# The second FFN product of a two-layer diffusion backbone as seven quarter products in place of eight

## The chip, the cores and the metric

The kernel runs on one core of a Trainium2 chip. The metric is device time in microseconds (us) of one execution. The kernel before takes 1958.51 us, the median of three runs (1956.71 to 1959.27).

An engine's name in the profile: PE is TensorE's matmuls, PEld its weight loads, DVE is VectorE, ACT is ScalarE, POOL is GpSimd, SP is the queue that issues the loads from device memory. L240 is line 240 of the kernel whose profile is shown.

## The reference

Two post-norm layers over 512 latent tokens (the second layer) or 512 latent and 256 context tokens (the first), with D = 1024. Each layer has a token mixer, gated linear attention in layer 0 and Mamba-2 in layer 1, and then an MLP with a squared ReLU, D_FF = 4096:

```python
def sq_relu_mlp(h, w1, w2):
    return jnp.square(jax.nn.relu(h @ w1)) @ w2
...
hl = layer_norm(DEEPNORM_ALPHA * hl + m_l[5] * sq_relu_mlp(modulate(hl, m_l[3], m_l[4]), ffn_w1[i], ffn_w2[i]),
                ln_g[i, 1], ln_b[i, 1])
```

`m_l` and `m_c` are rows of six modulation vectors ("ada"), a product of the conditioning vector with a matrix of 1024 x 6144 per layer. The change touches `@ w2` alone, in both layers.

## The kernel before

All data lie transposed: features on the 128 partitions, tokens along the columns. A tile of features is 128 of them, so D has 8 tiles and D_FF 32. A matmul takes a 128 x 128 block of weights and up to 512 token columns. In layer 0 the 768 tokens take two matmuls, of 512 and of 256 columns; in layer 1 the 512 tokens take one.

**Split products.** Every operand x is kept as two fp32r tensors, `xh` (x rounded by a cast on ScalarE) and `xl` (what is left, a subtraction on VectorE): `split_to`. A product is three matmuls, wh xh + wh xl + wl xh, all in line 240 (`prod`). Weights arrive in one of four buffers `raw` (512 KB, 128 x 1024 floats), and ScalarE's cast (L203) and VectorE's subtraction (L204) make `wh` and `wl`, three buffers each. The same four `raw` buffers serve W1, W2 and the ada matrix, taken in turn; a load is issued when the last reader of its buffer has ended.

**The FFN** (`ffn`, L363). An "f1 tile" is one of the 32 tiles of the first product, 8 x 3 matmuls per piece of tokens. Behind it come: relu out of PSUM on ScalarE (`rr`, L384), the square on GpSimd (`rq`, L385), the square's rounded part on ScalarE (`rh`, L386) and the rest on VectorE (`rl`, L387). The tiles of D_FF are then the k tiles of the second product. They are worked in five blocks of 8, 8, 8, 8 - n and n (n is 3 in layer 0, 2 in layer 1): all f1 tiles of a block, then for each of 8 output tiles the product with W2 over the block's k tiles and an addition of it, times the gate, to the residual `acc` in SBUF (`accum_proj`, VectorE, L419). The last n tiles go through `accum_last`, in pieces of 256 tokens, so that the layer norm of one piece overlaps the product of the next.

**What sets the order.** Each engine runs its instructions in the order of the program, and loads stand in one queue (SP). A scheduler that places the program's instructions by priority makes this order. Ada rows are spread over the other work: `worked` counts matmul columns, and after every `pace` units of 768 columns it advances `background` by a step, which loads 512 KB of the ada matrix and multiplies and sums them on VectorE (L157), once for the latent conditioning and, in the rows that the context needs too, a second time. The generators in `side` (layer norms) are advanced in the same way.

## Time and profile before

| | |
|---|---|
| median of the runs | 1958.51 us (1956.71 to 1959.27) |
| the profiled execution | span 1959.6 us |
| TensorE busy | 1881.3 us, 96% of the span |
| VectorE, ScalarE, GpSimd busy | 64%, 41%, 21% |
| bytes moved | 219.01 MB, 112 GB/s mean |
| FFN of layer 0, FFN of layer 1 | about 440 to 980 us; about 1600 to 1937 us |

The profiled execution is 1.1 us longer than the median. In the rows that follow, a group of instructions is given as: line, engine, operation, output<-inputs, their shapes, count | busy us, mean ns of one | idle time of the engine just ahead of them, and what ended it. In a timeline a row begins with the start in us from the span's start and the duration. The granted TensorE clock (PEclk) is 1.00 at full speed.

### The profile page before, as it was taken

The page shows a single profiled execution, that of the slowest core. Times are in us where ns is not written, and L with a number is a line of the kernel's source. Part 1 is how long each engine was busy: PE and PEld are TensorE (multiplying, and loading weights), DVE is VectorE, ACT ScalarE, POOL GpSimd, SP SyncE. Part 2 cuts the span into 40 slices and gives each one's busy share as a digit, 9 for nine tenths or more (in the row PEclk, how much of TensorE's full clock was granted, in tenths as well). Part 3 has the DMA queues.
Part 4 walks back from the last instruction along what each step waited for, and adds up shares of the span by engine and source line. Part 5 has one row for each costly group of instructions (what it writes and reads, how often), then busy time and mean ns, then how long its engine had stood idle before and what let it go on. Part 6 is the DMA issues. An engine that isn't in the chain of part 4 may idle for free.

```text
span 1959.6 us, 29026 instructions
## 1 busy us (share of the span) xinstructions
PE 1881.3 (96%) x11405; PEld 1604.9 (82%) x11405; DVE 1254.9 (64%) x1929; ACT 798.6 (41%) x1386; POOL 410.8 (21%) x448
## 2 busy tenths in 40 slices
...
GB/s 329 156 73 114 104 36 106 65 55 150 141 142 140 138 137 135 116 41 116 33 107 121 129 115 112 104 101 129 121 100 132 164 73 105 96 99 96 96 89 54
DMA packets 78936, 219.01 MB, mean 112 GB/s; under 512 B 11056, under 2 KB 15792, under 8 KB 78800
## 3 DMA queue, kind: packets, MB, share of 16 engines
...
## 4 chain that ended last, share of the span: by engine, by line
PE 63%; DVE 13%; DMA 7%; ACT 6%; POOL 5%; issue 5%; SPq 0%; DVEq 0%; POOLq 0%; ACTq 0%
PE mm L240 54%; DMA L<-crowc 4%; POOL L L1001 1%; ACT L L998 1%; DMA raw<-in_ada_wr_dram 1%; DVE A L593 1%; PE sm L943 1%; DVE raw L157 1%; DVE cv L867 1%; POOL L L912 1%; PE sm L676 1%; DVE wl L204 1%; POOL W L612 1%; PE sm L986 1%; PE mm L520 1%
## 5 line engine op out<-in xcount | busy, mean ns | idle before, releaser
L240 PE MATMUL mm<-xh,wh 128*128 128x512 f32 (+1 forms) x1824 | 554.2, 357 | 2.8 <-ACT xh L1044 2.6
L240 PE MATMUL mm<-xl,wh 128*128 128x512 f32 (+1 forms) x1824 | 550.0, 354 | 1.5 <-DVE xl L1045 1.5
L240 PE MATMUL mm<-xh,wl 128*128 128x512 f32 (+1 forms) x1824 | 549.7, 353 | 1.4 <-DVE wl L204 1.4
L203 ACT CAST wh<-raw 128x1024 fp32r<-128x1024 f32 (+3 forms) x227 | 227.8, 1004 | 658.5 <-PE mm L240 617.3
L204 DVE TENSOR_TENSOR wl<-raw,wh 128x1024 fp32r<-128x1024 f32 (+3 forms) x227 | 275.6, 1215 | 173.6 <-ACT wh L203 170.1
L240 PEld LDWEIGHTS mm<-xh,wh 128*128 128x128 f32 x1824 | 304.4, 189 | 54.4 <-ACT xh L1044 3.8
L240 PEld LDWEIGHTS mm<-xl,wh 128*128 128x128 f32 x1824 | 303.7, 189 | 50.6 <-issue 3.1
L240 PEld LDWEIGHTS mm<-xh,wl 128*128 128x128 f32 x1824 | 303.5, 189 | 50.7 <-DVE wl L204 2.5
L385 POOL TENSOR_TENSOR rq<-rr 128x768 f32<-128x768 f32 (+1 forms) x62 | 104.6, 1687 | 684.7 <-ACT rr L384 648.4
L240 PE MATMUL mm<-rl,wh 128*128 128x512 f32 x704 | 212.5, 355 | 3.8 <-DVE rl L387 3.8
L240 PE MATMUL mm<-rh,wl 128*128 128x512 f32 x704 | 212.4, 355 | 0.0
L240 PE MATMUL mm<-rh,wh 128*128 128x512 f32 x704 | 212.1, 355 | 0.0
L419 DVE SCALAR_TENSOR_TENSOR acc<-mm,row,acc 128x256 f32<-128x256 f32 (+1 forms) x182 | 100.7, 580 | 150.4 <-PE mm L240 150.0
L157 DVE SCALAR_TENSOR_TENSOR raw<-raw,srow 128x1024 f32<-128x1024 f32 x104 | 131.6, 1268 | 83.0 <-DMA raw<-in_ada_wr_dram 81.8
L867 DVE SCALAR_TENSOR_TENSOR cv<-pre,cvec,cv 128x770 f32<-128x770 f32 (+1 forms) x128 | 135.2, 1057 | 14.9 <-ACT cv L865 11.9
L240 PEld LDWEIGHTS mm<-rl,wh 128*128 128x128 f32 x704 | 116.0, 189 | 23.8 <-DVE rl L387 4.2
L240 PEld LDWEIGHTS mm<-rh,wh 128*128 128x128 f32 x704 | 116.1, 189 | 19.6
L240 PEld LDWEIGHTS mm<-rh,wl 128*128 128x128 f32 x704 | 116.1, 189 | 19.6
L998 ACT ACTIVATE L<-L,lcol 128x128 f32<-128x128 f32 x256 | 81.9, 393 | 69.1 <-POOL L L912 69.1
L387 DVE TENSOR_TENSOR rl<-rq,rh 128x768 fp32r<-128x768 f32 (+2 forms) x67 | 53.2, 794 | 64.0 <-POOL rq L385 63.7
L912 POOL TENSOR_SCALAR_AFFINE_SELECT L<-L 128x512 f32<-128x512 f32 x64 | 52.2, 817 | 142.5 <-DMA L<-crowc 141.4
L869 ACT ACTIVATE cf<-cv 128x512 f32<-128x512 f32 (+1 forms) x56 | 27.6, 533 | 86.5 <-DVE cv L867 86.5
...
## 6 DMA issues: line engine op xcount, KB each, us to landing
raw<-in_ffn_w_dram SPq DMA_DIRECT2D x112, 512.0 KB, 3.8
raw<-in_ada_wr_dram SPq DMA_DIRECT2D x80, 512.0 KB, 3.7
raw<-in_ssd_w_in_dram SPq DMA_DIRECT2D x48, 512.0 KB, 3.9
...
raw<-in_ada_w_dram SPq DMA_DIRECT2D x16, 512.0 KB, 9.1
raw<-in_gla_w_in_dram SPq DMA_DIRECT2D x16, 512.0 KB, 3.7
...
```

The source lines that it names most:

```text
L157: nc.vector.scalar_tensor_tensor(o, raw, 1.0, srow[s], ALU.mult, ALU.mult, accum_out=t[:, b, s:s + 1])
L203: nc.scalar.copy(h, src)
L204: nc.vector.tensor_sub(l, src, h.bitcast(F32))
L240: nc.tensor.matmul(part_of(ps, t0, n), a[:, k, :], b[:, t0:t0 + n], start=(k == 0 and i == 0), stop=(k == kt - 1 and i == 2))
L385: eng.tensor_mul(q[:, a:b], r[:, a:b], r[:, a:b])
L387: nc.vector.tensor_sub(rl[:, a:b], q[:, a:b], rh[:, a:b].bitcast(F32))
L419: nc.vector.scalar_tensor_tensor(acc[m][:, t0:t0 + n], part_of(ps, t0, n), gate[:, m, s:s + 1], (src or acc)[m][:, t0:t0 + n], ALU.mult, A ...
L520: nc.tensor.matmul(ps[:, 256 * tt:256 * tt + 256], a, b, start=(k == 0 and i == 0), stop=(k == KT - 1 and i == 2))
L867: nc.vector.scalar_tensor_tensor(c[:, 0:n], pre[:, t:t + n], cw(t), c[:, 0:n], ALU.mult, ALU.add)
L869: nc.scalar.activation(f[:, t0:t1], c[:, t0 + d:t1 + d], AF.Tanh)
L912: nc.gpsimd.affine_select(out=L[z], in_=L[z], compare_op=ALU.is_ge, fill=NEG, base=0, pattern=[[0, 4], [1 - 2 * z, P]], channel_multiplier ...
L998: nc.scalar.activation(t[:, h, :], t[:, h, :], AF.Exp, bias=lcol[:, c, r:r + 1])
```

## The change

W2's product is computed by Strassen's scheme in Winograd's form. The factors are cut into quarters: W2 over pairs of k tiles and pairs of output tiles, the squares over the same pairs of k tiles and two halves of the tokens. Seven products of quarters then replace eight; sums of quarters are needed on both sides, and each product is added to one, two or three quarters of the output.

- **Squares.** `square` (L400) writes two f1 tiles into one tile `F` of eight slots of half the tokens (384 columns in layer 0, 256 in layer 1); there is one such tile. GpSimd squares (L410) and makes four further slots by subtractions (L413 to L416). `combine` splits seven slots into `Rh` and `Rl`, by three casts and three subtractions.
- **Weights.** `quad_weights` makes three further blocks per four of W2 on GpSimd (L485 sub, L486 add in place, L487 sub, then L496 in layer 1 or L499 in layer 0), casts them on ScalarE and subtracts on VectorE (`wxh`, `wxl`, L480). In layer 1 (block of 8 k tiles) the two output tiles' weights are two `raw` buffers; in layer 0 (blocks of 4) one.
- **Products.** `quads` runs seven products per pair of output tiles (L528), 384 or 256 columns a matmul, and adds (L535) seven times per pair, in layer 0 with the second half in two parts, 128 latent and 256 context tokens.
- **Blocks.** Layer 0: seven of 4 k tiles and 4 in the closing part. Layer 1: 8, 8, 8, 6 and 2.
- **Order.** Ada products, splits and weight sums are marked `behind`: not issued before the last addition to the residual that stands ahead of them in the program. `pace` is 30 ahead of layer 0's FFN and 12 in both, and the matmuls of `quads` do not count. The layer-norm vectors `gb` are loaded where `F` was, ahead of the closing part.

```diff
+    def behind():
+        return tc.issue_after(ref[0].ins) if ref[0] else nullcontext()
...
-                    nc.vector.scalar_tensor_tensor(o, raw, 1.0, srow[s], ALU.mult, ALU.mult, accum_out=t[:, b, s:s + 1])
+                    with behind():
+                        nc.vector.scalar_tensor_tensor(o, raw, 1.0, srow[s], ALU.mult, ALU.mult, accum_out=t[:, b, s:s + 1])
...
-    def worked(cols):
+    def worked(cols, behind=True):
         clock[0] += cols
         while clock[0] >= UNIT:
             clock[0] -= UNIT
-            clock[1] += 1
+            clock[1] += behind
             wait[0] -= 1
             if wait[0] <= 0:
                 wait[0] = advance(side) or 1
-            if clock[1] % pace[0] == 0:
+            if behind and clock[1] % pace[0] == 0:
...
-        for bi, nb in enumerate((8, 8, 8, 8 - nlast, nlast)):
...
-            if bi < 4:
-                accum_proj(W2, h0, nb, ys, gate, acc, segs)
-            else:
-                accum_last(ws, ys, gate, acc, passes, after, early=None if layer == 0 else 5)
...
+        hn = NN // 2
+        kb = 4 if layer == 0 else 8
+        nlast = 4 if layer == 0 else 2
+        pend = []
+
+        def square(m, ps):
+            e = m % 2
+            r = pool.tile([P, NN], F32, tag="rr", name=nm("rr"), bufs=2)
+            for (t0, n, _) in segs:
+                nc.scalar.activation(r[:, t0:t0 + n], part_of(ps, t0, n), AF.Relu)
+            if e == 0:
+                pend.append(pool.tile([P, 8, hn], F32, tag="F", name=nm("F"), bufs=1))
+            F = pend[-1]
+            q = F[:, 0:2] if e else F[:, 6:8]
+            r = r.rearrange("p (a t) -> p a t", a=2)
+            nc.gpsimd.tensor_mul(q, r, r)
+            if e and m < DFF // P - nlast:
+                sub = nc.gpsimd.tensor_sub
+                sub(F[:, 2], F[:, 7], F[:, 6])
+                sub(F[:, 3], F[:, 1], F[:, 7])
+                sub(F[:, 4], F[:, 1], F[:, 2])
+                sub(F[:, 5], F[:, 0], F[:, 4])
...
+        def combine():
+            F = pend.pop(0)
+            h, l = (pool.tile([P, 7, hn], F32R, tag="R", name=nm(n), bufs=kb) for n in ("Rh", "Rl"))
+            for a, b in ((5, 7), (0, 3), (3, 5)):
+                split_to(h[:, a:b], l[:, a:b], F[:, a:b])
+            return h, l
...
+        def quad_weights(i, k0, nb):
+            kh = nb // 2
+            n = nb * P
+            one = 2 * n <= D
+            ts = [wpool.tile([P, KT, P], F32R, tag=t, name=nm(t), bufs=3) for _ in range(1 if one else 2) for t in ("wh", "wl")]
+            if one:
+                raw = raw_tile()[:, 0:2 * n].rearrange("p (m k n) -> p m k n", m=2, n=P)
+                nc.sync.dma_start(raw, W2[2 * i:2 * i + 2, :, k0:k0 + nb, :].rearrange("m p k n -> p m k n"))
+                e, o = raw[:, 0], raw[:, 1]
+                (eh, el), (oh, ol) = ([t[:, nb * j:nb * j + nb] for t in ts] for j in range(2))
+            else:
+                e, o = (wload(W2[2 * i + j][:, k0:k0 + nb, :]) for j in range(2))
+                (eh, el), (oh, ol) = ([t[:, 0:nb] for t in ts[2 * j:2 * j + 2]] for j in range(2))
+            xh, xl = (pool.tile([P, 1024 if layer == 0 else 1536], F32R, tag="wx", name=nm(t),
+                                bufs=4)[:, 0:3 * kh * P].rearrange("p (a k n) -> p a k n", a=3, n=P) for t in ("wxh", "wxl"))
+            t = wt_tile(kh)
+            inplace = t.shape[1] == 2
+            a11, a12, a21, a22 = e[:, 0::2], e[:, 1::2], o[:, 0::2], o[:, 1::2]
+            def cast(h, l, src):
+                nc.scalar.copy(h, src)
+                return lambda: nc.vector.tensor_sub(l, src, h.bitcast(F32))
+
+            subs = []
+            if not one:
+                subs.append(cast(eh, el, e))
+            nc.gpsimd.tensor_sub(t[:, 0], a11, a21)
+            nc.gpsimd.tensor_add(a21, a21, a22)
+            nc.gpsimd.tensor_sub(t[:, 1], a21, a11)
+            if one:
+                subs.append(cast(ts[0][:, 0:2 * nb], ts[1][:, 0:2 * nb], raw.rearrange("p m k n -> p (m k) n")))
+            else:
+                subs.append(cast(oh, ol, o))
+            if inplace:
+                subs.append(cast(xh[:, 0:2], xl[:, 0:2], t))
+                for f in subs[0:1]:
+                    f()
+                nc.gpsimd.tensor_sub(a12, a12, t[:, 1])
+                subs = [lambda: None] + subs[1:] + [cast(xh[:, 2], xl[:, 2], a12)]
+            else:
+                nc.gpsimd.tensor_sub(t[:, 2], a12, t[:, 1])
+                subs.append(cast(xh, xl, t))
...
+        def quads(k0, nb, R, gate):
+            kh = nb // 2
+            todo = []
+
+            def product(w, slot, ps, fresh):
+                for j in range(kh):
+                    (wh, wl), (Rh, Rl) = w[j], R[j]
+                    for x, (a, b) in enumerate(((wh, Rh), (wh, Rl), (wl, Rh))):
+                        nc.tensor.matmul(ps[:, 0:hn], a, b[:, slot], start=fresh and j + x == 0,
+                                         stop=j == kh - 1 and x == 2, skip_group_check=not fresh)
+                        worked(hn, False)
+
+            def add(m, half, ps):
+                o = 0
+                for (t0, n, s) in halves[half]:
+                    ref[0] = nc.vector.scalar_tensor_tensor(acc[m][:, t0:t0 + n], ps[:, o:o + n], gate[:, m, s:s + 1],
+                                                            acc[m][:, t0:t0 + n], ALU.mult, ALU.add)
+                    o += n
+
+            def last_product():
+                if todo:
+                    w, a, m = todo.pop()
+                    product(w["A22"], 5, a, False)
+                    add(m, 0, a)
+
+            for i in range(KT // 2):
+                e, o = 2 * i, 2 * i + 1
+                w = nxw.pop()[0]
+                a, c = bank(), sm_ps([P, 512])
+                product(w["A11"], 6, a, True)
+                add(e, 0, a)
+                d = sm_ps([P, 512])
+                product(w["A12"], 0, d, True)
+                add(e, 0, d)
+                if i < KT // 2 - 1:
+                    with behind():
+                        nxw.append(quad_weights(i + 1, k0, nb))
+                        cut = len(nxw[0][1]) // 2
+                        subtract(*nxw[0][1][:cut])
+                product(w["S1"], 2, c, True)
+                add(o, 1, c)
+                product(w["S2"], 4, a, False)
+                add(e, 1, a)
+                if i < KT // 2 - 1:
+                    with behind():
+                        subtract(*nxw[0][1][cut:])
+                last_product()
+                for x in (0, 1) if i < KT // 2 - 1 else (1, 0):
+                    product(w["S3" if x else "S4"], 3 if x else 1, a if x else c, False)
+                    add(o if x else e, 1, a if x else c)
+                todo.append((w, a, o))
...
+        nbs, left = [], DFF // P - nlast
+        while left:
+            nbs.append(min(kb, left))
+            left -= nbs[-1]
...
+        pace[0] = 12
+        for nb in nbs:
+            R = []
+            for p in range(nb // 2):
+                with behind():
+                    R.append(combine())
+                for m in range(ahead, ahead + 2):
+                    f1_square(m)
+                    if p == nb // 2 - 1 and m == ahead + (layer == 1):
+                        with behind():
+                            nxw.append(quad_weights(0, h0, nb))
+                            subtract(*nxw[0][1])
+                ahead += 2
+            if h0 == 0:
                 gate = mod(layer, 5)
-            if bi < 4:
-                accum_proj(W2, h0, nb, ys, gate, acc, segs)
-            else:
-                accum_last(ws, ys, gate, acc, passes, after, early=None if layer == 0 else 5)
+            quads(h0, nb, R, gate)
             h0 += nb
+        plain()
+        ready()
+        ws = pair_weights(W2, h0, nlast, ws_tiles)
+        for m in range(ahead, DFF // P):
+            f1(m, segs)
+        accum_last(ws, [rs[m] for m in range(nlast)], gate, acc, passes, after, early=None if layer == 0 else 5)
...
-        pace[0] = 21
+        pace[0] = 30
```

In the changed kernel, W1's cast and subtraction are L209 and L210, relu is L404, the ada product L163, W1's matmuls L246.

**Order on GpSimd, layer 1.** Numbers in names count buffers. Before, in the second product's neighbourhood GpSimd's program has only the squares:

```order
L385 TENSOR_TENSOR rq_2343_15704<-rr_2342_15703 128x512
L385 TENSOR_TENSOR rq_2351_15743<-rr_2350_15742 128x512
L385 TENSOR_TENSOR rq_2359_15782<-rr_2358_15781 128x512
L385 TENSOR_TENSOR rq_2367_15821<-rr_2366_15820 128x512
L385 TENSOR_TENSOR rq_2375_15860<-rr_2374_15859 128x512
```

In the changed kernel, from the third f1 tile of the second block of layer 1 on:

```order
L410 TENSOR_TENSOR F_2405_16429<-rr_2404_16427 128x512
L413 TENSOR_TENSOR F_2405_16429<-F_2405_16429 128x256
L485 TENSOR_TENSOR wt_2445_16641<-raw_2441_16635,raw_2442_16637 128x512
L486 TENSOR_TENSOR raw_2442_16637<-raw_2442_16637 128x4x128
L487 TENSOR_TENSOR wt_2445_16641<-raw_2442_16637,raw_2441_16635 128x512
L410 TENSOR_TENSOR F_2405_16429<-rr_2410_16462 128x512
L414 TENSOR_TENSOR F_2405_16429<-F_2405_16429 128x256
L415 TENSOR_TENSOR F_2405_16429<-F_2405_16429 128x256
L416 TENSOR_TENSOR F_2405_16429<-F_2405_16429 128x256
L410 TENSOR_TENSOR F_2418_16510<-rr_2417_16508 128x512
L413 TENSOR_TENSOR F_2418_16510<-F_2418_16510 128x256
L485 TENSOR_TENSOR wt_2457_16693<-raw_2453_16687,raw_2454_16689 128x512
```

Between two squares of one tile `F` stand now a subtraction and three operations on W2's weights, which need a load.

**Order on SP and VectorE, layer 1, same block.** The loads of the changed kernel, W1's last four and W2's first four; buffers of `raw` go round in fours, so `raw_2442` takes the buffer of `raw_2419`, `raw_2454` that of `raw_2432`:

```order
L233 DMA raw_2413_16477<-in_ffn_w1_dram 128x1024
L233 DMA raw_2419_16512<-in_ffn_w1_dram 128x1024
L233 DMA raw_2426_16558<-in_ffn_w1_dram 128x1024
L233 DMA raw_2432_16593<-in_ffn_w1_dram 128x1024
L233 DMA raw_2441_16635<-in_ffn_w2_dram 128x1024
L233 DMA raw_2442_16637<-in_ffn_w2_dram 128x1024
L233 DMA raw_2453_16687<-in_ffn_w2_dram 128x1024
L233 DMA raw_2454_16689<-in_ffn_w2_dram 128x1024
```

VectorE, the subtractions that free those buffers:

```order
L210 TENSOR_TENSOR Rl_2399_16389<-F_2392_16348,Rh_2398_16388 128x768
L210 TENSOR_TENSOR Rl_2399_16389<-F_2392_16348,Rh_2398_16388 128x512 x2
L210 TENSOR_TENSOR wl_2421_16515<-raw_2419_16512,wh_2420_16514 128x1024
L210 TENSOR_TENSOR wl_2428_16561<-raw_2426_16558,wh_2427_16560 128x1024
L480 TENSOR_TENSOR wxl_2444_16640<-wt_2445_16641,wxh_2443_16639 128x1024
L210 TENSOR_TENSOR Rl_2412_16470<-F_2405_16429,Rh_2411_16469 128x768
L210 TENSOR_TENSOR Rl_2412_16470<-F_2405_16429,Rh_2411_16469 128x512 x2
L210 TENSOR_TENSOR wl_2434_16596<-raw_2432_16593,wh_2433_16595 128x1024
L480 TENSOR_TENSOR wl_2438_16632<-raw_2441_16635,wh_2437_16631 128x1024
```

The subtraction that frees a buffer of W1 stands behind those of the tile `R` before it, and from there on behind those of W2's sums.

**Order on VectorE and ScalarE, layer 0.** Before, one ada product stands between the additions for two output tiles:

```order
L419 SCALAR_TENSOR_TENSOR acc_431_3248<-mm_905_6353,row05_4603,acc_431_3248 128x512
L419 SCALAR_TENSOR_TENSOR acc_431_3248<-mm_906_6354,row05_4603,acc_431_3248 128x256
L204 TENSOR_TENSOR wl_923_6539<-raw_921_6536,wh_922_6538 128x1024
L157 SCALAR_TENSOR_TENSOR raw_944_6739,row13_6517<-raw_944_6739,srow0_4597 128x1024
L419 SCALAR_TENSOR_TENSOR acc_432_3251<-mm_912_6417,row05_4603,acc_432_3251 128x512
L419 SCALAR_TENSOR_TENSOR acc_432_3251<-mm_913_6418,row05_4603,acc_432_3251 128x256
L204 TENSOR_TENSOR wl_929_6600<-raw_927_6597,wh_928_6599 128x1024
```

In the changed kernel, the second block: after the last addition of the first block come the splits of `R` and eight ada products, before the next W1 subtraction.

```order
L210 TENSOR_TENSOR Rl_753_5307<-F_705_4943,Rh_752_5306 128x768
L210 TENSOR_TENSOR Rl_753_5307<-F_705_4943,Rh_752_5306 128x1152
L210 TENSOR_TENSOR Rl_753_5307<-F_705_4943,Rh_752_5306 128x768
L163 SCALAR_TENSOR_TENSOR junk_760_5348,row10_5022<-raw_759_5346,srow0_4615 128x1024
L163 SCALAR_TENSOR_TENSOR junk_762_5377,row10_5022<-raw_761_5375,srow0_4615 128x1024
L163 SCALAR_TENSOR_TENSOR raw_759_5346,row10_5022<-raw_759_5346,srow1_4616 128x1024
L163 SCALAR_TENSOR_TENSOR raw_761_5375,row10_5022<-raw_761_5375,srow1_4616 128x1024
L163 SCALAR_TENSOR_TENSOR junk_771_5419,row10_5022<-raw_770_5417,srow0_4615 128x1024
L163 SCALAR_TENSOR_TENSOR junk_773_5448,row10_5022<-raw_772_5446,srow0_4615 128x1024
L163 SCALAR_TENSOR_TENSOR raw_770_5417,row10_5022<-raw_770_5417,srow1_4616 128x1024
L163 SCALAR_TENSOR_TENSOR raw_772_5446,row10_5022<-raw_772_5446,srow1_4616 128x1024
L210 TENSOR_TENSOR wl_779_5470<-raw_777_5467,wh_778_5469 128x1024
```

And ScalarE in the same block, W1's casts `wh_778` (third f1 tile) and `wh_795` (fourth):

```order
L209 CAST wh_778_5469<-raw_777_5467 128x1024
L404 ACTIVATE rr_774_5451<-mm_768_5391 128x512
L404 ACTIVATE rr_774_5451<-mm_769_5392 128x256
L209 CAST Rh_775_5459<-F_764_5383 128x1152
L209 CAST Rh_775_5459<-F_764_5383 128x768 x2
L479 CAST wh_788_5538<-raw_790_5540 128x1024
L479 CAST wxh_791_5542<-wt_793_5544 128x768
L209 CAST wh_795_5555<-raw_794_5553 128x1024
```

The cast of the fourth f1 tile's weights stands behind those of `R` and of W2's first weights, `wh_788` and `wxh_791`. `raw_790`, W2's first load, takes the buffer of the ada load `raw_772`, and `raw_772` that of `raw_759`.

110 lines of the change are left out of this document (76 added, 34 removed).

## The prediction

> **What bounds the kernel now.** I read the page first: busy time and the chain that ended last.
>
> ```profile
> span 1959.6 us, 29026 instructions
> PE 1881.3 (96%) x11405; PEld 1604.9 (82%) x11405; DVE 1254.9 (64%) x1929; ACT 798.6 (41%) x1386; POOL 410.8 (21%) x448
> PE 63%; DVE 13%; DMA 7%; ACT 6%; POOL 5%; issue 5%; SPq 0%; DVEq 0%; POOLq 0%; ACTq 0%
> L240 PE MATMUL mm<-rl,wh 128*128 128x512 f32 x704 | 212.5, 355 | 3.8 <-DVE rl L387 3.8
> ```
>
> The average mixes stages, so next the windows of the two FFNs: 200 us of layer 0, 200 us of layer 1, and three stretches that hold one kind of product (columns: busy time of each engine, clock, DMA share, GB/s).
>
> ```profile
> core 0: us, PE busy (x) PEld busy (x) DVE busy (x) ACT busy (x) POOL busy (x), PEclk, DMA share, GB/s
> 600.00:800.00 200.00, 200.00 (x1155) 174.86 (x1154) 91.29 (x121) 48.16 (x67) 25.36 (x14) 1.00 0.43 135
> 783.00:842.00 59.00, 59.00 (x342) 51.52 (x342) 21.36 (x31) 8.12 (x8) 0.00 (x0) 1.00 0.33 103
> 1600.00:1800.00 200.00, 200.00 (x903) 166.51 (x902) 76.51 (x87) 66.91 (x91) 34.05 (x21) 1.00 0.31 95
> 1650.00:1687.00 37.00, 37.00 (x165) 30.62 (x164) 13.60 (x14) 6.93 (x7) 0.00 (x0) 1.00 0.32 97
> ```
>
> In both FFNs TensorE is busy for every microsecond, at the full clock; no other engine reaches half. Of the second product TensorE waited once, 3.8 us for `rl`. So matmuls taken out here are time taken out, as long as nothing else becomes late. That is the whole question.
>
> **What is removed.** A 512-column matmul takes 37.0/165 = 0.224 us, a pair of 512 and 256 columns 59.0/171 = 0.345 us. The count of a window leaves out those that began before it, so I take 0.227 and 0.347; the difference, 0.120, is a 256-column matmul, and halfway between 256 and 512 columns a 384-column one is 0.1735.
> - Layer 0: before, 29 k tiles x 8 output tiles x 3 pairs = 241.5 us. After, 28 tiles in 7 blocks; a block has 4 pairs of output tiles, 7 products, 2 pairs of k tiles, 3 matmuls of 384: 168 x 7 x 0.1735 = 204.0. One tile more in the closing part, where tokens go in pieces of 256: 24 x 3 x 0.120 = 8.6. Balance -28.9.
> - Layer 1: before, 30 x 8 x 3 x 0.227 = 163.4; after, 15 pairs x 4 x 7 x 3 = 1260 matmuls x 0.120 = 151.2. Balance -12.2. The gain is small because two 256-column matmuls (0.240) cost more than one of 512.
> - The 3.8 us wait belongs to a product that is replaced: I take it out and count the new waits whole.
>
> Together -44.9 us, if TensorE never waits.
>
> **What is added, and its prices.** Rows of the FFN of layer 1, then of layer 0, then the nearest rows for a GpSimd operation that reads two different tensors:
>
> ```profile
> L204 DVE TENSOR_TENSOR wl<-raw,wh 128x1024 fp32r<-128x1024 f32 x53 | 64.9, 1225 | 71.7 <-ACT wh L203 68.9
> L203 ACT CAST wh<-raw 128x1024 fp32r<-128x1024 f32 x53 | 55.9, 1055 | 191.2 <-PE mm L240 191.2
> L385 POOL TENSOR_TENSOR rq<-rr 128x512 f32<-128x512 f32 x31 | 48.6, 1567 | 284.6 <-ACT rr L384 283.0 <-DVE rl L387 1.7
> L387 DVE TENSOR_TENSOR rl<-rq,rh 128x512 fp32r<-128x512 f32 x31 | 21.5, 693 | 34.5 <-POOL rq L385 34.5
> L384 ACT ACTIVATE rr<-mm 128x512 f32<-128x512 f32 x31 | 18.2, 591 | 8.8 <-PE mm L240 8.8
> ...
> L157 DVE SCALAR_TENSOR_TENSOR raw<-raw,srow 128x1024 f32<-128x1024 f32 x56 | 72.9, 1302 | 80.5 <-DMA raw<-in_ada_wr_dram 80.0
> L387 DVE TENSOR_TENSOR rl<-rq,rh 128x768 fp32r<-128x768 f32 x31 | 29.6, 956 | 29.2 <-POOL rq L385 29.2
> L419 DVE SCALAR_TENSOR_TENSOR acc<-mm,row,acc 128x256 f32<-128x256 f32 x40 | 18.9, 475 | 1.9 <-PE mm L240 1.9
> L203 ACT CAST ws<-raw 128x768 fp32r<-128x768 f32 x4 | 3.3, 834 | 8.2 <-DMA raw<-in_ffn_w_dram 8.2
> ...
> L284 POOL TENSOR_TENSOR xf<-xf,gb 128x512 f32<-128x512 f32 x3 | 3.8, 1271 | 0.6 <-ACT xf L283 0.6
> ```
>
> The square's mean of 1567 ns is not its cost. These timeline rows (start, duration) show a square alone, and two meetings of GpSimd and VectorE:
>
> ```profile
> 1927.96 1.04 POOL L385 TENSOR_TENSOR rq<-rr 128x512 f32<-128x512 f32 x1 [36.33 <-ACT rr L384]
> ...
> 1715.91 1.23 DVE L204 TENSOR_TENSOR wl<-raw,wh 128x1024 fp32r<-128x1024 f32 x1 [2.59 <-ACT wh L203]
> 1716.44 1.59 POOL L385 TENSOR_TENSOR rq<-rr 128x512 f32<-128x512 f32 x1 [3.85 <-ACT rr L384]
> ...
> 593.55 1.54 POOL L385 TENSOR_TENSOR rq<-rr 128x768 f32<-128x768 f32 x1 [6.39 <-ACT rr L384]
> 593.69 2.48 DVE L204 TENSOR_TENSOR wl<-raw,wh 128x1024 fp32r<-128x1024 f32 x1
> ```
>
> A square that meets nothing takes 1.04 us. One that starts 0.53 after a VectorE subtraction takes 1.59, and a subtraction that starts 0.14 after a square takes 2.48 in place of 1.23: whichever comes second waits until the other has ended. So a VectorE operation with two operands in SBUF and a GpSimd operation exclude each other, and their times add.
>
> The Trainium skill says the same (SBUF — State Buffer, "Who interferes with whom"): the port pair that both use is locked for a whole instruction. It speaks against this change, which puts most of its new work on just these two engines; the two meetings above agree with it. What hangs on it: without the lock the port waits in the steps of layer 1 below (0.6, 1.6, 0.3, 0.6) would go, 3.1 of the first wait's 5.2.
>
> Prices for what follows. GpSimd: square 1.04 (512 columns), 1.54 (768). A subtraction reads two different tensors: 1.26 at 512 by L284 (the largest price), 1.04 if it costs what a square does (the smallest). At 256 columns half of 1.26 and a tenth of fixed cost, since VectorE's 693 for half of 1225 leaves 0.08: 0.73; at 384, 0.99. VectorE: 1.23 (1024), 1.35 (1152, scaled), 0.95 (768), 0.69 (512); ScalarE: cast 1.05, 0.83, 0.62. A 512 KB load lands 3.7 after issue:
>
> ```profile
> raw<-in_ffn_w_dram SPq DMA_DIRECT2D x112, 512.0 KB, 3.8
> ```
>
> New work in a full block of layer 1 (8 k tiles; TensorE 8 x 24 x 0.227 + 336 x 0.120 = 83.9 us): GpSimd 8 squares, 16 subtractions of 256, 16 operations on weights of 512: 8.3 + 11.7 + 20.2 = 40.2. VectorE with two SBUF operands: 16 splits of 1024 and 4 of 512 for weights (22.5), 4 of 1024 for the weight sums (4.9), 7 slots x 4 pairs of squares (7.6, with the pieces as ordered): about 37. Sum 77 of 83.9 on one port: it fits, but 92% full, and in strict order on both engines. A block of 4 in layer 0 (62.4 us) has GpSimd 25, VectorE 37 with the 16 ada products of the early blocks: 62, full. So waits must be worked out along the order.
>
> **Layer 1, second block.** Zero is the start of its first f1 tile; one lasts 24 x 0.227 = 5.45. The second ends at 10.9.
> 1. A W1 cast stands ahead of its relu on ScalarE: 10.9 + 1.05 + 0.59 = 12.5. GpSimd: square into `F_2392` 1.57 (behind a split), three subtractions 2.2, one port wait 0.6: 17.0. Cast, two subtractions of `Rl_2399`, `wl_2421`: 20.2. That frees the buffer for `raw_2442`; it lands at 23.9.
> 2. GpSimd stands before L485, which needs it: three weight operations, 3.8, with the port: 28.0. Only then the square of `rr_2410` (ready since 22): 29.0; three subtractions and 1.6 of port waits (`wxl_2444` is in there): 32.8. Two casts, the cast `wh_2433`, `wl_2434`: 36.2. That frees the buffer for `raw_2454`: 39.9.
> 3. GpSimd again: three weight operations 44.0 (port waits included), square 45.0, two subtractions 46.5, L496 with a wait 48.4, one more 49.1, cast of `Rh_2424` 49.8.
>
> TensorE has done the 8 tiles at 43.6 and reaches `Rh_2424` 1 us later, 44.6: it waits 5.2. With 1.04 in place of 1.26 it is 2.7. I take 4. A second wait follows inside the products by the same turn (`wl_2440` frees `raw_2466`, three weight operations, four on `F_2431`, L496, cast, `wxl_2456`): the weights of the second pair of output tiles come some 5 late at the larger price; I take 4.5. The third pair, 2.7 late, and small ones, 2: 4.5 together. That makes 13 in a full block, 39 in three, and 9 in the block of six: 48. Bounds: 60 at the larger price, with 15 a block; 0 if the 7% of free port time absorbs all.
>
> **Layer 0, second block.** f1 tiles last 24 x 0.347 = 8.3; the fourth needs `wh_795` at 25.0. VectorE: adds and `Rl_753` until 4.5, three ada products 8.1; this frees the buffer of `raw_772`, landed 11.8; three more, 15.4; `raw_790` landed 19.1. The second tile's square is done at 19.2. GpSimd to L416 of `F_764`: 0.73 + 0.99 + 0.99 + 0.73 + 0.99, with two ada products in between, 26.0. ScalarE: `Rh_775` 2.9, `wh_788` 1.05, `wxh_791` 0.83, then `wh_795` 1.05: 31.8, 6.8 late. `wl_796`, behind five other subtractions, is another 1.7 to 2 later. So 8.5 for each of blocks 2 and 3. The first block starts without tiles ahead, while the rest of layer norm runs and its gate row is due: nearest is the same chain, of which two tiles are late; I take 15 (between 0 and 18). From block 4 the ada products are 8 in place of 16 and port time is free: 1.5 each, 6 in four. Together 38; bounds 0 and 50.
>
> What is moved at no cost: the load of `gb` goes ahead of the closing part, under 24 products and more; the ada rows come at another pace, and the last of them is due before the FFN of layer 1.
>
> **Sum.** -44.9 + 48 + 38 = +41 on the profiled 1959.6 is 2000.7; that execution is 1.1 above the median shown, so 2000 us.
>
> **Rivals.**
> - TensorE stays the bound and everything new hides: 1958.5 - 41 to 45, about 1915. For it: every window above has TensorE at 100% and GpSimd at 13 to 17%. Against: the turns above need every buffer, and the four `raw` buffers are the same ones. It is right if `Rh_2424` is cast before 44.6.
> - GpSimd is quicker than its rows, at about 0.7 of them. In steps 2 and 3 of layer 1 the six weight operations then lose 6 x 1.26 x 0.3 = 2.3, the two squares and six subtractions 2.0: the first wait of 4 goes. The others have fewer GpSimd operations in their turns and lose less; I put it at half of the 86 that stays, 43. That cancels the gain: about 1958, within 1940 to 1970. Against it: VectorE's subtraction at 593.69 itself waited 1.25, as long as the square's row says.
> - Worse than forecast: every wait at the larger price, 60 + 50 - 45 = +65, so 2024, and more if the adds, 20 us of VectorE per block of layer 0, hold PSUM banks. It decides if port waits in layer 1 exceed 2 us per pair of f1 tiles.
>
> The Trainium skill (Perfetto Trace Analysis, "GPSIMD Engine Instruction") counsels not to trust a GpSimd span but start-to-start spacing; by it the second rival would be likelier. No run here shows the two to differ.
>
> **How the numbers follow.** Forecast (with its own range of 1975 to 2032) 0.58; much worse, over 2032, 0.07; quicker GpSimd 0.17, of which 0.07 below, 0.05 within and 0.05 above 0.2% (about what a measurement tells from no change); TensorE bound 0.18. Faster 0.25, same 0.05, slower 0.70. The range 1930 to 2034 leaves out most of the TensorE-bound case and the worst: about 0.2.
>
> **What would show it.** In the profile after, TensorE's waits in the FFN should be some 80 to 90 us: in layer 1 under casts and subtractions of `Rh`, `wxh`, `wxl` (some 13 per 84 us block), in layer 0 under W1's `wh` and `wl` in the first three blocks. GpSimd's idle time ahead of L485 should be ended by loads of `raw`. VectorE's mean for a 1024 split should rise above 1225, and GpSimd's for a 256 subtraction above 0.8 us. If TensorE's idle stays under 20 us, port and order were misjudged; if most of it lies in layer 0, the ada products were undervalued.

## The result and the profile after

The changed kernel takes 2023.42 us (2016.28 to 2029.87), the kernel before 1957.95 us: a ratio of 1.0321, 95% interval 1.029 to 1.0353. It is 65 us slower; 2000 us was forecast, with a range of 1930 to 2034. The profiled execution took 2029.87 us, with a span of 2027.8 us.

The page of the changed kernel, its busy line, the chain that ended last, and the three TensorE groups with the longest idle time:

```profile
span 2027.8 us, 30683 instructions
PE 1878.4 (93%) x11801; PEld 1647.4 (81%) x11801; DVE 1514.5 (75%) x2335; ACT 865.9 (43%) x1469; POOL 748.1 (37%) x741
PE 51%; DVE 17%; POOL 13%; ACT 7%; DMA 7%; issue 6%; SPq 0%; POOLq 0%; DVEq 0%; ACTq 0%
L246 PE MATMUL mm<-xh,wh 128*128 128x512 f32 (+1 forms) x1824 | 558.2, 360 | 23.7 <-ACT wh L209 20.7
L528 PE MATMUL mm<-Rh,wh 128*128 128x256 f32 (+1 forms) x232 | 75.7, 326 | 27.3 <-ACT Rh L209 21.1
L528 PE MATMUL mm<-Rh,wxh 128*128 128x256 f32 (+1 forms) x232 | 74.4, 321 | 16.9 <-DVE acc L535 16.9
```

TensorE's part of the chain fell from 63% to 51%, GpSimd's rose from 5% to 13%. Each kind of wait that was forecast has its row: W1's cast in layer 0 (20.7 us), the cast of `Rh` at the start of layer 1's products (21.1), and, inside them, an addition on VectorE that stands behind the split of `wxl` (16.9). TensorE's busy sum hardly fell, although the products cost less by the forecast's count (11801 shorter matmuls in place of 11405): a 256-column row behind a wait lasts 0.41 us where one at full rate lasts 0.28, as rows further down show.

The next windows show one block, from the end of a first wait to the end of the next: of layer 0 and of layer 1.

```profile
core 0: us, PE busy (x) PEld busy (x) DVE busy (x) ACT busy (x) POOL busy (x), PEclk, DMA share, GB/s
562.90:637.90 75.00, 66.93 (x360) 60.72 (x360) 65.71 (x96) 20.19 (x28) 38.02 (x28) 0.93 0.36 113
1775.00:1875.20 100.20, 89.24 (x528) 80.83 (x528) 51.53 (x64) 33.93 (x46) 48.46 (x40) 0.93 0.27 85
```

A block of layer 0 takes 75.0 us where its matmuls need 62.4, one of layer 1 100.2 where they need 83.9, and the granted clock is 0.93 in both.

Two parts of the program tell where the time went. "Layer 0" runs from the first transpose of the layer norm ahead of its FFN to the first transpose of `dT` in layer 1's mixer (L1002, before L802), "layer 1" from the last transpose of the layer norm ahead of its FFN to the first of the final one. Starts and ends are read from the traces' matmul records. "Idle" is what TensorE waited in the FFN and the layer norms at its edges. "Half rate" is what matmuls lost that followed each other too slowly without a wait (a 256-column one 0.213 us after the last, in place of 0.120). Both go by the starts of matmuls; the idle times in the rows of the profile go by their modelled ends and add up to less, 37.4 and 47.5 us in the changed kernel's two parts.

| us | before | changed |
|---|---|---|
| layer 0 | 600.4 | 617.7 |
| idle, half rate in it | 9.8, 7.7 | 42.4, 20.4 |
| layer 1 | 337.0 | 390.5 |
| idle, half rate in it | 2.6, 1.2 | 55.8, 14.1 |

The mixer between them differs by up to 15 us from one profiled execution to the next, also where its code is the same; small differences below are therefore read from the two parts and not from the totals. Runs that leave layer 0 as it is in the changed kernel have 615.2 to 617.7 us there, runs that leave layer 1 as it is 389.9 to 392.7.

**The turn of layer 1, as it happened.** GpSimd in the second block of layer 1, from the third weight operation of the first pair of output tiles on; then ScalarE and TensorE behind it (start, duration):

```profile
1751.71 1.29 POOL L487 TENSOR_TENSOR wt<-raw,raw 128x512 f32<-128x512 f32 x1
...
1765.32 1.29 POOL L485 TENSOR_TENSOR wt<-raw,raw 128x512 f32<-128x512 f32 x1 [1.46 <-DMA raw<-in_ffn_w_dram]
1766.69 1.29 POOL L486 TENSOR_TENSOR raw<-raw 128x512 f32<-128x512 f32 x1
1768.05 1.29 POOL L487 TENSOR_TENSOR wt<-raw,raw 128x512 f32<-128x512 f32 x1
1769.30 1.04 POOL L410 TENSOR_TENSOR F<-rr 128x512 f32<-128x512 f32 x1
1770.42 0.73 POOL L414 TENSOR_TENSOR F<-F 128x256 f32<-128x256 f32 x1
...
1771.79 1.97 POOL L496 TENSOR_TENSOR raw<-raw,wt 128x512 f32<-128x512 f32 x1
1773.72 0.72 POOL L416 TENSOR_TENSOR F<-F 128x256 f32<-128x256 f32 x1
```

```profile
1774.47 1.14 ACT L209 CAST Rh<-F 128x512 fp32r<-128x512 f32 x2 [3.27 <-POOL F L416]
...
1769.35 0.28 PE L528 MATMUL mm<-Rh,wl 128*128 128x256 f32 x1
1775.14 0.58 PE L528 MATMUL mm<-Rh,wh 128*128 128x256 f32 x1 [5.52 <-ACT Rh L209]
```

TensorE ended the block's eight f1 tiles at 1768.4, which the forecast put at 43.6, so its zero is 1724.8. On that scale L487 ended at 28.2 (forecast 28.0), the second L485 began at 40.5 (39.9), the last subtraction ended at 49.6 (49.1), and TensorE waited 5.5 us (5.2 at the larger price). In this kernel a weight operation of 512 columns that meets nothing takes 1.29 us and a subtraction of 256 takes 0.73.

### The profile page after: what moved, and what is told of

Same layout as the page of the kernel before. It is cut to its first block, busy times and chain, and to the rows that moved or that the text cites. A ratio compares the mean times of both kernels' runs of the same rounds, so it can differ in the third digit from the quotient of the medians.

```text
span 2027.8 us, 30683 instructions
## 1 busy us (share of the span) xinstructions
PE 1878.4 (93%) x11801; PEld 1647.4 (81%) x11801; DVE 1514.5 (75%) x2335; ACT 865.9 (43%) x1469; POOL 748.1 (37%) x741
## 4 chain that ended last, share of the span: by engine, by line
PE 51%; DVE 17%; POOL 13%; ACT 7%; DMA 7%; issue 6%; SPq 0%; POOLq 0%; DVEq 0%; ACTq 0%
PE mm L246 28%; PE mm L528 8%; PE sm L528 6%; DMA L<-crowc 3%; DMA raw<-in_ffn_w_dram 2%; DVE cv L1067 2%; DVE wl L210 2%; POOL raw L486 1%; POOL F L410 1%; DVE raw L163 1%; ACT wh L209 1%; DVE A L793 1%; POOL wt L485 1%; POOL wt L487 1%; POOL F L415 1%
## 5 line engine op out<-in xcount | busy, mean ns | idle before, releaser
L246 PE MATMUL mm<-xh,wh 128*128 128x512 f32 (+1 forms) x1824 | 558.2, 360 | 23.7 <-ACT wh L209 20.7
L246 PE MATMUL mm<-xh,wl 128*128 128x512 f32 (+1 forms) x1824 | 555.0, 356 | 6.6 <-DVE wl L210 6.6
L246 PE MATMUL mm<-xl,wh 128*128 128x512 f32 (+1 forms) x1824 | 553.9, 356 | 1.2 <-DVE xl L1245 1.1
L246 PEld LDWEIGHTS mm<-xh,wh 128*128 128x128 f32 x1824 | 307.9, 191 | 76.0 <-ACT wh L209 22.0
L246 PEld LDWEIGHTS mm<-xh,wl 128*128 128x128 f32 x1824 | 306.8, 191 | 57.8 <-DVE wl L210 9.5
L246 PEld LDWEIGHTS mm<-xl,wh 128*128 128x128 f32 x1824 | 306.7, 191 | 51.1 <-issue 3.1
L210 DVE TENSOR_TENSOR wl<-raw,wh 128x1024 fp32r<-128x1024 f32 (+3 forms) x163 | 209.5, 1287 | 81.5 <-ACT wh L209 80.8
L209 ACT CAST wh<-raw 128x1024 fp32r<-128x1024 f32 (+3 forms) x163 | 164.4, 1010 | 211.8 <-PE mm L246 94.1
L410 POOL TENSOR_TENSOR F<-rr 128x512 f32<-128x512 f32 (+1 forms) x62 | 101.8, 1642 | 319.1 <-DVE raw L163 154.8
L210 DVE TENSOR_TENSOR Rl<-F,Rh 128x768 fp32r<-128x768 f32 (+2 forms) x87 | 93.0, 1105 | 85.6 <-ACT Rh L209 85.4
L1067 DVE SCALAR_TENSOR_TENSOR cv<-pre,cvec,cv 128x770 f32<-128x770 f32 (+1 forms) x128 | 136.4, 1066 | 14.9 <-ACT cv L1065 13.2
L163 DVE SCALAR_TENSOR_TENSOR raw<-raw,srow 128x1024 f32<-128x1024 f32 x104 | 145.2, 1418 | 2.7 <-DMA raw<-in_ada_wr_dram 2.1
L535 DVE SCALAR_TENSOR_TENSOR acc<-mm,row,acc 128x256 f32<-128x256 f32 (+2 forms) x232 | 104.9, 478 | 47.1 <-PE mm L528 46.3
L209 ACT CAST Rh<-F 128x768 fp32r<-128x768 f32 (+2 forms) x87 | 68.3, 812 | 125.7 <-POOL F L410 34.2
L528 PE MATMUL mm<-Rh,wh 128*128 128x256 f32 (+1 forms) x232 | 75.7, 326 | 27.3 <-ACT Rh L209 21.1
L480 DVE TENSOR_TENSOR wl<-raw,wh 128x1024 fp32r<-128x1024 f32 (+1 forms) x60 | 80.7, 1348 | 17.0 <-ACT wh L479 16.7
L535 DVE SCALAR_TENSOR_TENSOR acc<-sm,row,acc 128x256 f32<-128x256 f32 (+2 forms) x188 | 80.7, 457 | 15.3 <-PE sm L528 13.7
L479 ACT CAST wxh<-wt 128x768 fp32r<-128x768 f32 (+1 forms) x44 | 39.3, 893 | 120.5 <-POOL wt L487 49.6
L528 PE MATMUL mm<-Rh,wxh 128*128 128x256 f32 (+1 forms) x232 | 74.4, 321 | 16.9 <-DVE acc L535 16.9
```

Source lines behind the costliest of these rows:

```text
L163: nc.vector.scalar_tensor_tensor(o, raw, 1.0, srow[s], ALU.mult, ALU.mult, accum_out=t[:, b, s:s + 1])
L209: nc.scalar.copy(h, src)
L210: nc.vector.tensor_sub(l, src, h.bitcast(F32))
L246: nc.tensor.matmul(part_of(ps, t0, n), a[:, k, :], b[:, t0:t0 + n], start=(k == 0 and i == 0), stop=(k == kt - 1 and i == 2))
L410: nc.gpsimd.tensor_mul(q, r, r)
L479: nc.scalar.copy(h, src)
```

## The experiments

All are edits of the changed kernel; e7 computes something else and counts for its time alone. Times are medians; a ratio is to the kernel before on the same chip, whose median lay between 1957.95 and 1962.65 us.

| kernel | us | ratio (95%) | layer 0 | layer 1 |
|---|---|---|---|---|
| before | 1957.95 | | 600.4 | 337.0 |
| changed | 2023.42 | 1.0321 (1.029 to 1.0353) | 617.7 | 390.5 |
| e1 order in layer 1 | 1996.74 | 1.0201 (1.0169 to 1.0234) | 615.8 | 364.4 |
| e2 sums on VectorE | 1963.99 | 1.0021 (1.0003 to 1.0039) | 616.8 | 329.1 |
| e3 fillers, both waits | 2022.39 | 1.0332 (1.0299 to 1.0364) | 615.2 | 390.7 |
| e4 layer 0's weights later | 2012.53 | 1.0285 (1.0253 to 1.0317) | 607.0 | 392.7 |
| e5 all edits | 1937.56 | 0.988 (0.9851 to 0.991) | 589.4 | 330.6 |
| e6 seven products in layer 1 alone | 1955.52 | 0.9965 (0.9943 to 0.9987) | 599.5 | 328.7 |
| e7 half of the double ada products | 1995.0 | 1.016 (1.0126 to 1.0194) | 586.0 | 391.3 |
| e8 fillers, second wait | 2026.98 | 1.0348 (1.0316 to 1.0379) | 616.1 | 392.1 |
| e9 fillers, layer 0 | 2030.59 | 1.0361 (1.0309 to 1.0413) | 620.5 | 389.9 |

### e1: the same work in another order

`sq` collects the last subtraction of each pair of squares, `lastw` the last weight operation of each pair of output tiles.

```diff
+        def later():
+            return tc.issue_after(sq[-2].ins) if layer else nullcontext()
...
-            nc.gpsimd.tensor_sub(t[:, 0], a11, a21)
+            if layer and lastw:
+                with tc.issue_after(lastw[-1].ins):
+                    nc.gpsimd.tensor_sub(t[:, 0], a11, a21)
...
-                        with behind():
+                        with behind(), later():
                             nxw.append(quad_weights(0, h0, nb))
```

> Edit: in layer 1 GpSimd's three weight operations of the first pair of output tiles stand behind the last subtraction of the last pair of squares that the block's products need, and those of the next pair behind them. Same instructions, same durations, same load on the shared port. Theory A (the waits come from the turn in GpSimd's order: squares stand behind weight sums that wait for a load): the first wait of each block of layer 1 (5.6 to 8.6 us, ended by the cast of Rh) goes to under 1; the waits inside the products become smaller, about 9 a block in place of 11; the time falls by 25 to 35 us, half of it idle time and the rest the half-rate matmuls behind it. Theory B (the port is 92% full, whatever the order): the wait only changes its place; within 8 us of the changed kernel.

27 us faster than the changed kernel; layer 1's part fell from 390.5 to 364.4. TensorE's groups in e1's layer 1:

```profile
L536 PE MATMUL mm<-Rh,wh 128*128 128x256 f32 x117 | 34.0, 291 | 0.3 <-ACT wh L483 0.3
L536 PE MATMUL sm<-Rh,wl 128*128 128x256 f32 x120 | 35.5, 296 | 7.6 <-DVE wl L484 7.6
L536 PE MATMUL sm<-Rh,wxh 128*128 128x256 f32 x57 | 18.2, 319 | 11.5 <-DVE acc L543 11.5
```

The wait for `Rh` is gone (21.1 to 0.3), with every instruction still there and as much work on the port. What remains stands inside the products. So the first wait came from a place in GpSimd's order, as theory A has it; a full port alone would have kept it. Layer 1's part is still 27 us longer than before the change.

### e2: layer 1's weight sums on VectorE

```diff
-            nc.gpsimd.tensor_sub(t[:, 0], a11, a21)
-            nc.gpsimd.tensor_add(a21, a21, a22)
-            nc.gpsimd.tensor_sub(t[:, 1], a21, a11)
+            (nc.vector if layer else nc.gpsimd).tensor_sub(t[:, 0], a11, a21)
+            (nc.vector if layer else nc.gpsimd).tensor_add(a21, a21, a22)
+            (nc.vector if layer else nc.gpsimd).tensor_sub(t[:, 1], a21, a11)
...
-                nc.gpsimd.tensor_sub(a12, a12, t[:, 1])
+                (nc.vector if layer else nc.gpsimd).tensor_sub(a12, a12, t[:, 1])
```

> Edit: layer 1's weight sums (four operations of 512 columns per pair of output tiles) on VectorE in place of GpSimd. Takes 20 us of GpSimd per full block and adds 11 us on VectorE. Theory A (turn and GpSimd's slowness): loads are waited for by VectorE after its own splits, a sum takes 0.69 us and not 1.27, nothing stands between the squares: waits of layer 1 fall from 52 to under 12 us, the half-rate stretches with them; the time falls by 50 to 65 us, to about 1960 to 1970. Rival (VectorE, with 61 us of 84 in a block before, becomes the bound and the additions to the residual come late): faster by less than 20, with waits ended by additions (L535) of more than 25 us.

59 us faster than the changed kernel. e2's layer 1: two of the moved operations, the only larger wait that is left on TensorE, and 200 us of it:

```profile
L485 DVE TENSOR_TENSOR wt<-raw,raw 128x512 f32<-128x512 f32 x12 | 9.2, 766 | 11.7 <-DMA raw<-in_ffn_w_dram 11.7
L486 DVE TENSOR_TENSOR raw<-raw 128x512 f32<-128x512 f32 x12 | 11.1, 925 | 0.1
...
L528 PE MATMUL sm<-Rh,wxh 128*128 128x256 f32 x60 | 17.4, 290 | 2.8 <-DVE acc L535 2.8
...
1700.00:1900.00 200.00, 198.16 (x1197) 177.85 (x1196) 140.97 (x181) 81.25 (x106) 72.44 (x60) 1.00 0.29 95
```

With the sums away from GpSimd TensorE is busy for 198 of 200 us at the full clock. Layer 1's part is 329.1 us, 7.9 below the kernel before, against 12.2 us of matmuls saved. VectorE did not become the bound at 141 of 200. The loads are the same, and so are the four `raw` buffers; they alone do not hold the block. This edit changes the place of the sums and their price at once; e1 shows what the place alone is worth, the price alone was not measured.

### e3 and e8: does the half rate behind a wait cost time?

```diff
+            def filler(ps, a, b, n):
+                for _ in range(n):
+                    nc.tensor.matmul(ps[:, 0:hn], a, b, start=True, stop=True)
...
                 a, c = bank(), sm_ps([P, 512])
+                if layer and nb == 8 and i == 0:
+                    filler(a, w["A11"][0][0], R[0][0][:, 6], 40)
                 product(w["A11"], 6, a, True)
...
+                if layer and nb == 8 and i == 1:
+                    filler(sm_ps([P, 512]), w["A11"][0][0], R[0][0][:, 6], 40)
                 product(w["S2"], 4, a, False)
```

> Edit: in the three blocks of 8 of layer 1, 40 matmuls of 256 columns whose output is thrown away (4.8 us of TensorE) ahead of the first product of the block, and 40 ahead of the product at which the second wait stands. They fill the waits. If a wait costs only its idle time, the time stays within 3 us (longer by what the fillers exceed the waits). If the wait also halves the rate of the matmuls behind it (213 in place of 120 ns for 3 to 5 us in the profile), six such stretches of about 1.6 to 2.4 us go: 9 to 14 us faster.

The changed kernel's matmuls behind a wait, second block of layer 1:

```profile
1776.25 0.41 PE L528 MATMUL mm<-Rh,wl 128*128 128x256 f32 x1
1776.46 0.41 PE L528 MATMUL sm<-Rh,wh 128*128 128x256 f32 x1
1776.68 0.41 PE L528 MATMUL sm<-Rl,wh 128*128 128x256 f32 x1
1776.89 0.41 PE L528 MATMUL sm<-Rh,wl 128*128 128x256 f32 x1
```

They start 0.21 us apart, for 17 matmuls in a row, and then 0.12 again. The Trainium skill (TensorE: Matmul & The Clock Gate, "Wait — 56ns, not 53.3ns?") gives a cold array N / 1.2 GHz from start to start, 0.213 for 256 columns; these rows agree. The loss of six such stretches was expected back, 9 to 14 us. It did not come: the time and layer 1's part (390.7 against 390.5) are as they were, although in the second block of layer 1 no half-rate stretch is left and TensorE's waits of more than 0.4 us are 0.66, 0.69 and 1.89 us. From its first filler to the first filler of the block behind it are 1758.90 to 1858.21, 99.3 us, where the same block took 100.2 without fillers. Over layer 1, idle, half rate and fillers together are 30.2 + 10.9 + 28.8 = 69.9 us, as much as idle and half rate before (55.8 + 14.1). The fillers took the place of the waits, and the block kept its length.

The chain that ended last agrees for this block. In the changed kernel it leaves TensorE at 1746.6 us, passes through casts, splits, loads and GpSimd, and comes back to TensorE only at 1806.5; both slow stretches (1775.9 to 1779.8 and 1794.6 to 1800.3) lie between (start, duration, what; "issue" is time for which the profile shows no wait):

```profile
1734.78 11.80 PE mm L246 x52
1746.61 1.06 ACT wh L209
...
1780.92 1.63 issue
1782.59 1.31 POOL wt L485
1783.97 2.17 POOL raw L486
...
1806.51 1.45 PE sm L528 x10
```

e8 fills the second wait alone, in another bank. Its expectation starts from a misreading of e3: there too the fillers at this place ran at once, 1779.72 to 1784.68, and what I took for the rest of the second wait stands one pair of output tiles later.

```diff
+                if layer and nb == 8 and i == 1:
+                    filler(bank(), w["A11"][0][0], R[0][0][:, 6], 40)
                 product(w["S2"], 4, a, False)
```

> Edit, on the changed kernel: 40 matmuls of 256 columns into a PSUM bank that is free (their output is thrown away) ahead of the product at which the second wait of a block of 8 of layer 1 stands (4.8 of 5.2 us); the first wait is left as it is. In e3 the fillers at this place had to wait for a bank, and the half-rate matmuls stayed. Theory A (layer 1's turn is set by GpSimd and loads, and half-rate matmuls ahead of the next wait cost nothing; behind the second wait they push the next block back): the stretches behind the second waits go and layer 1's part, 390.5 us, becomes 4 to 8 us shorter. Rival 1 (they cost nothing anywhere in layer 1): 390.5 within 2. Rival 2 (the rate does not depend on the wait being filled): the stretches stay, and so does the time.

The second waits of the three blocks were filled, and layer 1's part became 392.1 us, within the spread of the runs that leave layer 1 as it is; waits of 1.9 to 2.2 us stand one pair of output tiles later in each block, as in e3. In two of the three blocks a slow stretch came back behind that wait, so e8 took little half rate away, and the stronger test is e3's second block: some 4 us of it gone, 0.9 us won. Together with the chain this speaks for rival 1: the length of layer 1's block is set by GpSimd, the loads and VectorE, and TensorE's rate inside it costs next to nothing on top.

### e4 and e7: layer 0

```diff
-                    if p == nb // 2 - 1 and m == ahead + (layer == 1):
+                    if p == nb // 2 - 1 and m == ahead + 1:
                         with behind():
                             nxw.append(quad_weights(0, h0, nb))
```

> Edit: in layer 0 the first weights of a block's products are asked for after the block's fourth f1 tile and not after the third, so that W1's load and casts for the fourth tile stand ahead of them on SP, ScalarE and VectorE. Theory A (the fourth tile waits since its cast stands behind W2's weights, which wait for a buffer that ada products hold): the 6.6 and 1.5 us waits of blocks 2 and 3 fall to 1 and some 3 us come back at the start of the products; waits in layer 0 fall by 5 to 9 us, the half-rate stretches of 2 blocks go (4 us): 8 to 14 us faster. Rival (VectorE is simply full with ada products in these blocks, whatever the order): the wait moves to the products, within 3 us.

11 us faster than the changed kernel, layer 0's part 617.7 to 607.0; idle time in it is 30.0 us. The 6.5 us waits for the fourth tile's cast (6.6 in the expectation) are gone; some 3 us came back at the start of the products.

e7 leaves out the first of the two products of each ada row that is needed twice:

```diff
-                for s in streams:
+                for s in (streams if not fewer[0] else streams[-1:]):
```

> Edit, on the changed kernel: of the ada rows that are multiplied twice (24 loads in layer 0's FFN), one of the two products is left out, so those rows are wrong. VectorE has 8 ada products a block in blocks 1 to 3 in place of 16; loads and their order are as they were. Theory A: the chain of blocks 2 and 3 (splits, 3 + 3 ada products between two loads, then GpSimd) loses some 4 us and its port waits: the 6.6 us waits for W1's cast of the fourth tile fall under 2, the first block's also, waits in layer 0 fall by 20 to 25 us; 20 to 30 us faster than the changed kernel. Rival (the casts of W2's weights hold the tile, whoever fills the port): the 6.6 us waits fall by less than 2, the time by less than 8 us.

28 us faster than the changed kernel; layer 0's part is 31.7 shorter. The same block as above, in the changed kernel 75.0 us long, in e7:

```profile
555.60:620.40 64.80, 63.06 (x362) 58.18 (x360) 52.12 (x80) 20.01 (x27) 34.44 (x29) 1.00 0.41 130
```

Eight ada products fewer in the block, 8 x 1.22 (one that meets nothing) = 9.8 us on VectorE, made it 10.2 shorter. So VectorE's ada products held this block. That the two numbers are so close shows no rate of one to one: at 64.8 us the block is near the 62.4 that its matmuls need, so a larger saving could not have shown, and in the changed kernel's block an ada product took 1.52 to 1.69 us on the mean, not 1.22. e4 shows that order has a share too. That the chain passes through VectorE's ada products several times is how the forecast worked it out, and both runs fit it.

### e9: fillers in layer 0

```diff
+            if layer == 0 and fill:
+                x = fill[0][0][:, 6]
+                for _ in range(48):
+                    nc.tensor.matmul(ps[0][:, 0:256], x[:, 0:P], x[:, 0:256], start=True, stop=True)
             prod(ps, w, xs, sg, KT)
```

> Edit, on the changed kernel: in the first three blocks of layer 0, 48 matmuls of 256 columns (output thrown away, 5.8 us of TensorE) ahead of the fourth f1 tile, where the 6.6 us waits for W1's cast stand. Layer 0's part, from the first transpose of the layer norm ahead of its FFN to the first matmul of layer 1's mixer, is 617.7 us in the changed kernel (615.7 to 617.7 in e1 to e3, which have the same layer 0). Theory A (in layer 0 a block's chain starts with the end of the products before it, so matmuls at half rate behind a wait push everything): the half-rate stretches behind the 6.6 us waits go, and the part becomes 4 to 8 us shorter. Rival (a chain that VectorE sets; TensorE's rate behind the wait is hidden): the part stays within 2, or is up to 3 longer since the fillers end later than the wait did.

Layer 0's part became 620.5 us, 2.8 longer, so the rival's end. But the half-rate matmuls did not go: behind the fillers of blocks 2 and 3 a wait of 3.1 us for W1's subtraction was left, and 15 or 16 matmuls after it were still slow. So e9 does not tell whether they cost time. The changed kernel's chain says that here they do; second block:

```profile
564.66 2.42 DVE wl L210
567.12 9.85 PE mm L246 x44
...
607.52 15.62 PE mm L246 x90
```

Behind the wait for `wl` the chain runs on TensorE. 44 matmuls (22 pairs) take 9.85 us there and would take 7.6 at 0.347 a pair, as the 90 later ones do (15.62 for 45 pairs). That is 2.2 us in this block, by the chain and not by an experiment.

### e6 and e5: versions that are a little faster than both

e6 has the old `ffn` and its `pace` for layer 0 and e2's `ffn` for layer 1.

```diff
-        ffn(0, us, acc, BOTH, fp, 2, CTXL0, L1, (CTX, L0, L1), after0)
+        ffn_plain(0, us, acc, BOTH, fp, 2, CTXL0, L1, (CTX, L0, L1), after0)
```

> Edit: layer 0's FFN as before the change (eight products); layer 1 with seven products and its weight sums on VectorE. Layer 1's part, from the last transpose of the layer norm ahead of its FFN to the first of the last one, was 337.0 us before the change and 329.1 in e2. If layers add up: 1950 to 1952, 0.35 to 0.45% faster than before. If the mixer or layer norm between them give it back: within 0.2%.

0.9965 (0.9943 to 0.9987): layer 1 alone is worth a third of a percent. e5 has e2's and e4's edits and these two, the first of which holds back all work on the later pairs' weights, not the casts alone:

```diff
-                    with behind():
+                    with behind(), tc.issue_after(relu[0].ins):
                         nxw.append(quad_weights(i + 1, k0, nb))
...
-        pace[0] = 12
+        pace[0] = 14
```

> Edits together: layer 1's weight sums on VectorE (as in e2); layer 0's first weights of a block after the fourth f1 tile (as in e4); the casts of the second and later pairs' weights on ScalarE behind the last relu of the block; an ada step every 14 units in the place of 12. The third edit is for 2.1 to 2.7 us waits that stand at the start of the products in blocks 4 to 7 of layer 0: there a relu, which frees the PSUM banks, stands behind a cast of weights that waits for GpSimd. Theory A (all waits come from places in the order): layer 0 keeps some 15 us of waits, layer 1 under 8; layer 0 about 10 us and layer 1 about 8 us shorter than before the change: 1940 to 1948. Rival (layer 0 is held by VectorE and the port being full, not by places): layer 0 not shorter than before the change, 1950 to 1958.

1937.56 us, 0.988 (0.9851 to 0.991), a little better than expected: layer 0 is 11.0 us and layer 1 6.4 us shorter than before the change. That is 17.4 of the 23 us that the ratio gives; the rest lies outside the two parts. Its busy line:

```profile
span 1940.8 us, 30593 instructions
PE 1852.6 (95%) x11801; PEld 1625.5 (84%) x11801; DVE 1546.8 (80%) x2399; ACT 868.9 (45%) x1469; POOL 680.7 (35%) x677
```

The seven products are there as in the changed kernel; the difference of 86 us is only where the added work stands, on which engine, and at which pace the ada rows come.

## Why the prediction was right, and where its size was off

**Sign and mechanism.** Slower, by the new work on GpSimd and VectorE and the order it stands in, not by TensorE. The profile shows the main waits where they were put, and e1, e2, e4 and e7 each take some of them away.

**TensorE's saving** (28.9 and 12.2 us). e2's layer 1 has next to no waits and is 7.9 us shorter than before. Its matmuls there take 5.2 us longer from start to start than 0.227 us for each of 512 columns and 0.120 for each of 256 would give, before the change 0.9: 7.9 + 4.3 = 12.2, as forecast. (The 0.227 is right, the reason given for it is not: 37.0/165 comes out at 0.224 because the count of a window takes in matmuls that only reach into it.) In layer 0 the saving was never free of waits, so its 28.9 is not shown alone; e5 reaches 11.0.

**The waits.** Forecast 48 us in layer 1 and 38 in layer 0; idle time grew by 55.8 - 2.6 = 53.2 and, with the old 3.8 us wait taken out, by 42.4 - 6.0 = 36.4. In layer 0 the 6.8 us wait for `wh_795` was 6.5 and the next one 1.2 where 1.7 to 2 were given. In layer 1 the agreement of the sum is in part luck. The first and second waits of a full block were longer than the 4 and 4.5 taken (5.5 and 5.0 in the second block, 8.4 at the start of the first), the third pair's and the smaller ones came to at most 1.1 us a block where 4.5 were taken, and of the 9 us in the block of six 6.0 stand at its last pair of output tiles.

**What was off.** The sum gave +41 and the result is +65. By the parts, 12 us are missing in layer 0 (17.3 measured, 38 - 3.8 - 28.9 = 5.3 forecast) and 18 in layer 1 (53.5 measured, 48 - 12.2 = 35.8 forecast); the rest of the program gives some back. The sum priced a wait as TensorE's idle time at one place and went on from there at full rate. It had no term for matmuls at half rate behind a wait, 12.7 us more of them in layer 0 and 12.9 in layer 1.
- Layer 1: "13 in a full block". The second block lost 100.2 - 83.9 = 16.3 us, some 12 idle and some 4 at half rate. By e3 and the chain, the half rate there takes up time that TensorE would otherwise have waited. What made the block longer than forecast is the turn behind the first wait. The first wait itself is explained by its price: "With 1.04 in place of 1.26 it is 2.7. I take 4" averaged the nearest row of the same two-tensor shape (1271 ns; the operations took 1.29) with one of another kind, and 5.2 at the larger price was right within 0.3. The next turn has two pieces in the chain above that the forecast does not name: 1.63 us ahead of L485 for which the chain names no releaser, and L486 at 2.17 us in place of 1.29. Together they are 2.5 us of the 3.3 that are missing in this block; that they are the cause is argued and was not tested.
- Layer 0: "8.5 for each of blocks 2 and 3". Each lost 75.0 - 62.4 = 12.6 us. The waits account for 8; the rest are matmuls at half rate behind them. By the chain 2.2 us of these count in the block's length; no run took them away and left the wait. The kernel before showed them behind its one wait, two matmuls (512 and 256 columns) every 0.64 us in place of 0.347:

```profile
513.63 1.01 PE L240 MATMUL mm<-rl,wh 128*128 128x512 f32 x2 [3.83 <-DVE rl L387]
514.44 0.84 PE L240 MATMUL mm<-rh,wl 128*128 128x512 f32 x2
515.08 0.84 PE L240 MATMUL mm<-rh,wh 128*128 128x512 f32 x2
```

That half rate grew by 25.6 us in the two parts, about as much as the forecast missed, is therefore no account of the miss by itself: in layer 1 it is another face of the same waits, in layer 0 a part of it is, by the chain, time lost.

**The rivals.** "TensorE stays the bound" is refuted for this order by the waits; e2 shows that it is reached in layer 1 once the sums are moved. "GpSimd is quicker than its rows" is refuted: L485 to L487 start 1.37 and 1.36 us apart at durations of 1.29. "Worse than forecast" gave 2024 us, and 2023.42 was measured, but that is luck: it rests on waits of 60 and 50 us, and 53 and 36 came.

**What would show it.** Waits of 80 to 90 us: 53 + 36 = 89. GpSimd's 256 subtraction above 0.8 us: 985 to 1066 ns for three of the four lines, 783 for L414. L485's idle time ended by loads, and VectorE's 1024 split above 1225 (layer 1 of the changed kernel):

```profile
L485 POOL TENSOR_TENSOR wt<-raw,raw 128x512 f32<-128x512 f32 x12 | 16.5, 1371 | 35.9 <-DMA raw<-in_ffn_w_dram 28.4 <-DVE wl L210 4.5 <-DVE acc L535 3.0
L210 DVE TENSOR_TENSOR wl<-raw,wh 128x1024 fp32r<-128x1024 f32 x29 | 37.0, 1279 | 33.9 <-ACT wh L209 33.9
```
